# The condition's product with the modulation weights, on VectorE or on four column tiles of TensorE

## The chip, the cores and the metric

The kernel runs on one core of one Trainium2 chip. The metric is the device time of one execution in microseconds (us); of several runs the median is taken. The engines are named as in the profile: PE is TensorE (PEld its weight loads), DVE is VectorE, ACT is ScalarE, POOL is GpSimd, SP is SyncE, whose queue issues most of the DMAs (SPq).

## What is computed

A two-layer trunk on 1024 frames of width 1024. Each layer has a mixer and a mixture of experts, and each of these is modulated by vectors that come from the condition `c`. Only this part of the reference bears on the change:

```python
cond = jax.nn.silu(c)                       # (1, 1024)
for i in range(2):
    shift1, scale1, gate1, shift2, scale2, gate2 = jnp.split(cond @ ada_w[i] + ada_b[i], 6, axis=-1)
    h = modulate(rmsnorm(x, norm_mix_w[i]), shift1, scale1)     # h * (1 + scale) + shift
    ...                                                         # mixer, experts
```

So there are twelve vectors of 1024 numbers, each the product of one vector of 1024 with a 1024 x 1024 block of float32 weights (4 MB): 48 MB of weights that are read once and used for one row.

## The kernel before, in words

`even` (line 1979) is layer 0 up to its experts. It goes through these stages, which overlap at their edges:

- **Start.** Four tiles of x are loaded, normed and transposed (`norm_S`, line 189). `ada` (line 142) makes scale1 and shift1 of layer 0 (line 2024). `modulate` (line 217) then writes the normed input as a high and a low part (hTh, hTl), and four more tiles follow.
- **Projections** (loop at line 2047, eight steps). Each step loads a block of `even_w_in`, splits it into a high and a low part (`wsplit`, line 228: ACT at line 138, then DVE at line 139) and multiplies it in three passes (`mm3`, lines 240 to 242). Within the steps n = 1 to 5, `ada` makes eight more vectors (line 2067): gate1, scale2, shift2, gate2 of layer 0 and shift1, scale1, gate1, scale2 of layer 1. A vector's loads and products are written into the code in one place and its last part (after the `yield` at line 169) at the next vector's place.
- **Stick-breaking attention and S5** (`stick`, line 283, and `s5_quad`, line 462), eight row blocks and four groups of channels.
- **GLU** (`glu`, line 586), with the last two vectors, shift2 and gate2 of layer 1 (line 2103), and some row blocks of `stick` beside it. Then the output projection and the routing.

`ada` takes each 1024 x 1024 block in four quarters h of 256 columns. `wload` (line 74) brings a quarter (1 MB) into a tile `w` of shape 128 x (8 row blocks k) x 256; its DMA is issued by SP. The tile comes from a ring of two buffers in the projection and GLU stages (`pick(1)`) and of four at the start, so a load waits in SP's queue until the products of an earlier quarter have read their buffer, and what stands behind it in that queue waits too. The products are made on DVE: one `tensor_scalar` (line 160) and seven `scalar_tensor_tensor` (line 167) that add w[:, k, :] times a column of `cs` (silu of c) into `adacc`, 128 x 256. After the `yield`, PE sums over the 128 partitions with `ones_f` (line 179, two products of one column for each quarter), DVE adds the bias (line 180), and for most vectors ACT's queue writes the result to DRAM (line 187). One quarter out of the eight at the start is done on PE instead, sixteen sums of eight products of one column each (`on_pe`, line 177).

The program is written with a tile framework. `tile.TileContext(nc, schedule_with_timeline_sim=True)` (in `kernel`) means that the order of the instructions on each engine is made by a planner that plays the program through on a simulated timeline and prefers work that stands earlier in the code; semaphores are put in by the framework. Each engine runs its list in order: an instruction that waits holds up all that stand behind it. `psum("e")` gives one of two PSUM banks that `ada`, `s5_quad` and `glu` share.

Of the kernel before, what the change touches and what calls it, by code (L numbers as in the profile page):

```python
# [9 lines left out]
FT = mybir.dt.float32  # L10
# [11 lines left out]
D = 1024  # L22
# [14 lines left out]
class Core:  # L37
# [41 lines left out]

    def consts(self):  # L80
        nc, c = self.nc, self.const
        ji = c.tile([128, 128], I32, name="ji")
        nc.gpsimd.iota(ji, pattern=[[1, 128]], base=0, channel_multiplier=-1)
        self.ident = c.tile([128, 128], FT, name="ident")
        nc.vector.tensor_scalar(self.ident, ji, 0.0, None, op0=OP.is_equal)
        self.ustrict = c.tile([128, 128], BF, name="ustrict")
        nc.vector.tensor_scalar(self.ustrict, ji, 0.0, None, op0=OP.is_gt)
        self.ones_b = c.tile([128, 128], BF, name="ones_b")
        nc.vector.memset(self.ones_b, 1.0)
        self.ones_f = c.tile([128, 128], FT, name="ones_f")  # L90
        nc.vector.memset(self.ones_f, 1.0)
        self.nhalf = c.tile([128, 16], FT, name="nhalf")
        nc.vector.memset(self.nhalf, -0.5)
        self.euler = c.tile([128, 4], FT, name="euler")
        nc.vector.memset(self.euler, math.e)
        self.eps = c.tile([128, 1], FT, name="eps")
        nc.vector.memset(self.eps, 1e-6)
        cr = c.tile([128, KD], FT, name="cr")
        nc.sync.dma_start(cr, self.a["c"][0].rearrange("(k p) -> p k", p=128))
        self.cs = c.tile([128, KD], FT, name="cs")  # L100
        nc.scalar.activation(self.cs, cr, AF.Silu)
        self.mod_d = self.dram.tile([2, 6, D], FT, name="mod_d")
        self.mod = {}

# [34 lines left out]
        self.nc.vector.tensor_tensor(lo, x, hi.bitcast(FT), op=OP.subtract)  # L139


    def ada(self, i, names, pool, tag, on_pe=((),), pool_eng=False):

        nc, a, c = self.nc, self.a, self.const
        order = ["shift1", "scale1", "gate1", "shift2", "scale2", "gate2"]
        aw, ab = a["ada_w"], a["ada_b"]
        for m, nm in enumerate(names):
            j = order.index(nm)
            b = self.col(pool, ab[i, j * D:(j + 1) * D], "adac", KD)
            keep = j < 2  # L150
            o = c.tile([128, KD], FT, name=f"{nm}_{i}") if keep else pool.tile([128, KD], FT, name="adao", bufs=2)
            parts = []
            for h in range(4):
                w = self.wload(aw[i, :, j * D + h * 256:j * D + (h + 1) * 256], 8)
                if h in on_pe[m % len(on_pe)]:
                    parts.append(w)
                    continue
                acc = pool.tile([128, 256], FT, name="adacc", bufs=4)
                eng = nc.gpsimd if pool_eng else nc.vector
                eng.tensor_scalar(acc, w[:, 0, :], self.cs[:, 0:1], None, op0=OP.mult)  # L160
                for k in range(1, KD):
                    wk, ck = w[:, k, :], self.cs[:, k:k + 1]
                    if pool_eng:
                        eng.tensor_scalar(wk, wk, ck, None, op0=OP.mult)
                        eng.tensor_tensor(acc, acc, wk, op=OP.add)
                    else:
                        eng.scalar_tensor_tensor(acc, wk, ck, acc, op0=OP.mult, op1=OP.add)  # L167
                parts.append(acc)
            yield
            pc = self.psum(tag)  # L170
            for h, x in enumerate(parts):
                for q in range(2):
                    qs = slice(q * 128, (q + 1) * 128)
                    p = pc[:, 2 * h + q:2 * h + q + 1]
                    if h in on_pe[m % len(on_pe)]:
                        for k in range(KD):
                            nc.tensor.matmul(p, x[:, k, qs], self.cs[:, k:k + 1], start=(k == 0), stop=(k == KD - 1))
                    else:
                        nc.tensor.matmul(p, x[:, qs], self.ones_f[:, 0:1], start=True, stop=True)
            nc.vector.tensor_tensor(o, pc[:, 0:KD], b, op=OP.add)  # L180
            if nm.startswith("scale"):
                n = self.col(pool, (a["norm_mix_w"] if nm == "scale1" else a["norm_ffn_w"])[i], "adan", KD)
                nc.vector.scalar_tensor_tensor(o, o, 1.0, n, op0=OP.add, op1=OP.mult)
            if keep:
                self.mod[nm, i] = o
            else:
                nc.scalar.dma_start(self.mod_d[i, j].rearrange("(k p) -> p k", p=128), o)
# [1791 lines left out]
    def even(self, x_src):  # L1979
# [9 lines left out]
        with self.banks("pse", b=4, a=1, d=1, e=2):  # L1989
# [16 lines left out]
            with tc.tile_pool(name="hT", bufs=1, side="right") as hp, tc.tile_pool(name="wsp", bufs=1, side="right") as wp:  # L2006
                hs = [hp.tile([128, KD, T], FR, name=n) for n in ("hTh", "hTl")]
                with tc.tile_pool(name="nrm", bufs=1, side="left") as np_:
# [12 lines left out]
                        load(t)  # L2021
                    pre = qT[:].rearrange("p h t -> p (h t)").rearrange("p (k t) -> p k t", k=KD)
                    self.norm_S(get, None, None, *hs, np_, "ad", range(4), eng=nc.gpsimd, pre=pre)
                    list(self.ada(0, ["scale1", "shift1"], ap, "e", ((2,), ())))
                    mod = self.mod["scale1", 0], self.mod["shift1", 0]
                    for h in range(2):
                        ts = slice(256 * h, 256 * h + 256)
# [157 lines left out]
```

## Time and profile before

| what | us |
|---|---|
| three runs, median (lowest to highest) | 3074.36 (3069.44 to 3075.93) |
| the profiled execution | 3069.93 |
| its span | 3068.1 |
| PE busy in the span | 2656.4 (87%) |
| DVE busy in the span | 1792.6 (58%) |

Between the span and the execution's own time lie 1.8 us. All of `ada` lies in the first 650 us of the span; the rest (the experts of layer 0, layer 1) uses its results only. The table shows averages over the whole span, so what bounds a stage has to be read from windows of the trace: for each stretch the busy time of each engine, the TensorE clock that was granted (1.00 is 2.4 GHz, 0.50 is 1.2 GHz) and the share of the DMA engines. A matmul in float32 stands in the trace as two entries, one for each of its passes; the duration of one entry reaches past the start of the next, so the pace is read from how far apart the starts lie.

### The profile page before, as it was taken

What the parts mean: (1) busy time and instruction counts of PE and PEld (TensorE: products, weight loads), DVE (VectorE), ACT (ScalarE), POOL (GpSimd) and SP (SyncE); (2) the same over time, 40 slices, a digit from 0 to 9 for tenths busy, and PEclk for the clock granted to TensorE, in tenths of its full rate; (3) what the DMA queues carried; (4) which work ended last, traced back from release to release, by engine and by line L of the source; (5) the groups of instructions that cost most, each with busy time, mean ns of one, the idle gap of its engine ahead of it and who ended that gap; (6) DMA issues with size and microseconds to landing.
All of it is one profiled execution on the core that took longest, in us unless ns stands there. A gap on an engine that the chain in (4) does not pass through costs nothing. (4 is left out here: it accounts for less than half of the span.)

```text
span 3068.1 us, 39923 instructions
## 1 busy us (share of the span) xinstructions
PE 2656.4 (87%) x14357; PEld 1854.7 (60%) x14357; DVE 1792.6 (58%) x3211; ACT 1120.7 (37%) x1777; POOL 831.2 (27%) x1157
## 2 busy tenths in 40 slices
PE   4987688989699999995799999999978799998991
PEld 4776466647444466662677777777877444566660
DVE  7546999655633477664734555646547434556664
ACT  4311456432232345552433323323233223345451
POOL 5260755324211031101301533354105111111101
PEclk9998689989799999997898978886988799999996
DMA  8746220223588899997745322244443689999995
GB/s 279 178 124 198 63 59 15 90 68 105 211 338 324 351 368 407 376 389 256 260 138 176 110 77 78 67 121 103 107 125 119 242 348 365 369 362 396 388 385 239
DMA packets 345018, 672.82 MB, mean 219 GB/s; under 512 B 118591, under 2 KB 259935, under 8 KB 293104
## 3 DMA queue, kind: packets, MB, share of 16 engines
q1 hardware_dynamic: 272960, 611.23, 54.7%
q10 hardware_dynamic: 56752, 25.41, 3.0%
q0 software_dynamic: 15104, 33.58, 3.0%
q8 instruction: 115, 1.88, 0.3%
q14 instruction: 87, 0.71, 0.1%
HBM read 611.31 MB, written 79.79 MB: 225 GB/s over the span
## 5 line engine op out<-in xcount | busy, mean ns | idle before, releaser
L139 DVE TENSOR_TENSOR wlo<-w,whi 128x1024 fp32r<-128x1024 f32 x384 | 451.4, 1220 | 114.0 <-ACT whi L138 112.3
L138 ACT ACTIVATE whi<-w 128x1024 fp32r<-128x1024 f32 x384 | 390.5, 1054 | 237.1 <-PE ps_g L839 69.9
L240 PE MATMUL ps_b<-hTh,wh 128*128 128x512 f32 x608 | 259.3, 428 | 28.2 <-ACT cc L1382 12.5
L241 PE MATMUL ps_b<-hTl,wh 128*128 128x512 f32 x608 | 255.2, 420 | 0.0
L242 PE MATMUL ps_b<-hTh,wl 128*128 128x512 f32 x608 | 254.8, 419 | 0.0
L788 POOL DMA_INDIRECT xg<-h_d,tok x56 | 80.6, 1440 | 641.6 <-PE ps_t L106 617.1
L847 DVE TENSOR_TENSOR hs<-hs,ps_u 128x512 f32<-128x512 f32 x48 | 32.9, 685 | 263.3 <-PE ps_u L917 212.4
L794 POOL DMA_INDIRECT ye_d<-y,tab x48 | 71.9, 1497 | 421.8 <-DVE y L856 328.4
L167 DVE SCALAR_TENSOR_TENSOR adacc<-w,cs,adacc 128x256 f32<-128x256 f32 x329 | 161.1, 507 | 5.2
L139 DVE TENSOR_TENSOR wl<-w,wh 128x1024 fp32r<-128x1024 f32 x84 | 104.0, 1253 | 97.3 <-ACT wh L138 88.1
L240 PEld LDWEIGHTS ps_b<-hTh,wh 128*128 128x128 f32 x608 | 124.8, 206 | 55.9 <-ACT cc L1382 13.3
L846 ACT ACTIVATE hs<-ps_g 128x512 f32<-128x512 f32 x48 | 28.7, 598 | 325.0 <-PE ps_g L917 244.8
L313 DVE TENSOR_TENSOR_SCAN sP<-keep,sP,sbz 128x256 f32<-128x256 f32 (+1 forms) x160 | 132.9, 874 | 21.7 <-POOL keep L307 10.5
L917 PE MATMUL ps_g<-w,xh 128*64 128x512 f32 x512 | 143.5, 598 | 0.0
L133 POOL TENSOR_TENSOR rs<-rm,nhalf 128x1 f32<-128x1 f32 (+2 forms) x56 | 49.9, 892 | 344.9 <-DVE rm L131 293.2
L138 ACT ACTIVATE wh<-w 128x1024 fp32r<-128x1024 f32 x84 | 86.3, 1053 | 150.5 <-PE ps_b L241 132.4
L241 PEld LDWEIGHTS ps_b<-hTl,wh 128*128 128x128 f32 x608 | 124.7, 205 | 27.2 <-DVE hTl L139 0.3
L242 PEld LDWEIGHTS ps_b<-hTh,wl 128*128 128x128 f32 x608 | 123.9, 204 | 28.3 <-issue 0.4
L917 PE MATMUL ps_u<-w,xh 128*64 128x512 f32 x512 | 137.6, 595 | 0.0
L315 POOL TENSOR_TENSOR sw<-sw,sP 128x512 f32<-128x512 f32 (+1 forms) x80 | 101.1, 1265 | 132.6 <-DVE sP L313 57.3
L926 PE MATMUL ps_y<-w,hh 128*64 128x512 f32 x512 | 122.0, 598 | 2.2 <-ACT hh L921 2.2
L1699 POOL TENSOR_TENSOR T<-N,X 128x60 f32<-128x60 f32 (+24 forms) x248 | 87.1, 351 | 125.2 <-DMA N<-n_d 93.3
(709 smaller groups left out, 6177.9 us busy)
## 6 DMA issues: line engine op xcount, KB each, us to landing
w<-in_moe_w_gate_dram SPq DMA_DIRECT2D x128, 1024.0 KB, 14.7
w<-in_moe_w_up_dram SPq DMA_DIRECT2D x128, 1024.0 KB, 14.8
w<-in_moe_w_down_dram SPq DMA_DIRECT2D x128, 1024.0 KB, 13.4
w<-in_ada_w_dram SPq DMA_DIRECT2D x48, 1024.0 KB, 5.8
w<-in_odd_w_in_dram SPq DMA_DIRECT2D x26, 1024.0 KB, 5.7
cy<-ye_d SPq DMA_DIRECT2D x16, 1024.0 KB, 10.8
cx<-xm_d SPq DMA_DIRECT2D x29, 512.0 KB, 7.5
w<-in_even_w_in_dram SPq DMA_DIRECT2D x8, 1024.0 KB, 8.5
```

What stands on the lines that cost most here:

```text
L138: self.nc.scalar.activation(hi, x, AF.Copy)
L139: self.nc.vector.tensor_tensor(lo, x, hi.bitcast(FT), op=OP.subtract)
L167: eng.scalar_tensor_tensor(acc, wk, ck, acc, op0=OP.mult, op1=OP.add)
L240: nc.tensor.matmul(p, a[0], b[0], start=first, stop=False)
L241: nc.tensor.matmul(p, a[0], b[1], start=False, stop=False)
L242: nc.tensor.matmul(p, a[1], b[0], start=False, stop=last)
L313: v.tensor_tensor_scan(P[:, r, 0:n][:, ::-1], keep[:, r, 0:n][:, ::-1], zero.to_broadcast([128, n]), P[:, r, n:n + 1], op0=OP.mult, op1=OP ...
L315: g.tensor_tensor(w[:, :, 0:n], w[:, :, 0:n], P[:, :, 1:n + 1], op=OP.mult)
L788: nc.gpsimd.indirect_dma_start(out=xg, out_offset=None, in_=h_d[:], in_offset=bass.IndirectOffsetOnAxis(ap=tokc, axis=0), bounds_check=T - ...
L917: nc.tensor.matmul(ps[z][r], x[:, 4 * h + k, r], w[z][h][:, k, :], start=(h == 0 and k == 0), stop=(h == 1 and k == 3))
L926: nc.tensor.matmul(py[n][r], ht[:, f, r], w[2][f // 2][:, f % 2, two[n]], start=(f == 0), stop=(f == 3))
L1699: g.tensor_tensor(o, N[:, 0:j, j:j + 1].to_broadcast([128, j, w]), X[:, j:j + 1, c:8].to_broadcast([128, j, w]), op=OP.mult)
```

## The change

The eight DVE instructions of a quarter go. In their place are eight matmuls on PE: the weights are `csz`, a new constant tile in which column 0 of 32 holds a column of `cs` and the others are zero, and the quarter's w[:, k, :] is the moving operand (256 columns). Row block k goes to the column tile k % 4 (`tile_position=(0, 32 * (k % 4))`), so that four row blocks write to four groups of 32 partitions of one PSUM bank, and k = 4 to 7 add to what k = 0 to 3 left. Two quarters share a bank (`pa`, from the same two banks "e"); ACT copies the bank to SBUF (`adacc`, now 128 x 512, two buffers in place of four of 128 x 256). The sum over partitions by `ones_f` stays as it was in kind, eight products of one column for each vector (now for all twelve vectors; `on_pe` is gone). The loads `w` and their rings stay.

```diff
     def consts(self):
-        ji = c.tile([128, 128], I32, name="ji")
+        self.ident = c.tile([128, 128], FT, name="ident")
+        ji = self.ident[:].bitcast(I32)
         nc.gpsimd.iota(ji, pattern=[[1, 128]], base=0, channel_multiplier=-1)
-        self.ident = c.tile([128, 128], FT, name="ident")
-        nc.vector.tensor_scalar(self.ident, ji, 0.0, None, op0=OP.is_equal)
         self.ustrict = c.tile([128, 128], BF, name="ustrict")
         nc.vector.tensor_scalar(self.ustrict, ji, 0.0, None, op0=OP.is_gt)
+        nc.vector.tensor_scalar(self.ident, ji, 0.0, None, op0=OP.is_equal)
...
+        self.csz = c.tile([128, KD, 32], FT, name="csz")
+        nc.vector.memset(self.csz, 0.0)
+        nc.vector.tensor_copy(self.csz[:, :, 0:1], self.cs[:, :, None])
...
-    def ada(self, i, names, pool, tag, on_pe=((),), pool_eng=False):
+    def ada(self, i, names, pool, tag):
...
             parts = []
-            for h in range(4):
-                w = self.wload(aw[i, :, j * D + h * 256:j * D + (h + 1) * 256], 8)
-                if h in on_pe[m % len(on_pe)]:
-                    parts.append(w)
-                    continue
-                acc = pool.tile([128, 256], FT, name="adacc", bufs=4)
-                eng = nc.gpsimd if pool_eng else nc.vector
-                eng.tensor_scalar(acc, w[:, 0, :], self.cs[:, 0:1], None, op0=OP.mult)
-                for k in range(1, KD):
-                    wk, ck = w[:, k, :], self.cs[:, k:k + 1]
...
-                        eng.scalar_tensor_tensor(acc, wk, ck, acc, op0=OP.mult, op1=OP.add)
+            for h2 in range(2):
+                pa = self.psum(tag)
+                for h in (2 * h2, 2 * h2 + 1):
+                    w = self.wload(aw[i, :, j * D + h * 256:j * D + (h + 1) * 256], 8)
+                    for k in range(KD):
+                        q = 32 * (k % 4)
+                        nc.tensor.matmul(pa[q:q + 32, h % 2 * 256:h % 2 * 256 + 256], self.csz[:, k, :], w[:, k, :],
+                                         start=(k < 4), stop=(k >= 4), tile_position=(0, q))
+                acc = pool.tile([128, 512], FT, name="adacc", bufs=2)
+                nc.scalar.activation(acc, pa, AF.Copy)
                 parts.append(acc)
             yield
             pc = self.psum(tag)
-            for h, x in enumerate(parts):
-                for q in range(2):
...
-                    if h in on_pe[m % len(on_pe)]:
-                        for k in range(KD):
-                            nc.tensor.matmul(p, x[:, k, qs], self.cs[:, k:k + 1], start=(k == 0), stop=(k == KD - 1))
-                    else:
-                        nc.tensor.matmul(p, x[:, qs], self.ones_f[:, 0:1], start=True, stop=True)
+            for n in range(KD):
+                nc.tensor.matmul(pc[:, n:n + 1], parts[n // 4][:, n % 4 * 128:n % 4 * 128 + 128], self.ones_f[:, 0:1], start=True, stop=True)
...
-                    list(self.ada(0, ["scale1", "shift1"], ap, "e", ((2,), ())))
+                    list(self.ada(0, ["scale1", "shift1"], ap, "e"))
```

## Rows read from the trace of the kernel before

**Rows 1.** The page's part 1: busy time, share of the span and instructions of each engine over the whole span.

```profile
PE 2656.4 (87%) x14357; PEld 1854.7 (60%) x14357; DVE 1792.6 (58%) x3211; ACT 1120.7 (37%) x1777; POOL 831.2 (27%) x1157
```

**Rows 2.** Busy time of each engine (x instructions) in six stretches that follow the stages, then granted clock, DMA share and GB/s. The number behind the stretch is its length.

```profile
core 0: us, PE busy (x) PEld busy (x) DVE busy (x) ACT busy (x) POOL busy (x), PEclk, DMA share, GB/s
0.00:60.00 60.00, 23.17 (x100) 20.51 (x100) 43.23 (x90) 24.33 (x40) 35.83 (x27) 1.00 0.96 314
60.00:285.00 225.00, 207.22 (x909) 170.35 (x909) 131.70 (x357) 47.44 (x60) 65.67 (x180) 0.94 0.64 170
285.00:300.00 15.00, 3.61 (x15) 2.25 (x14) 4.68 (x16) 1.02 (x1) 5.03 (x7) 0.66 0.55 64
300.00:330.00 30.00, 15.05 (x66) 9.40 (x66) 26.53 (x55) 9.22 (x17) 19.45 (x20) 0.50 0.52 141
330.00:550.00 220.00, 178.55 (x1250) 127.63 (x1250) 212.49 (x362) 124.79 (x265) 131.84 (x122) 0.87 0.15 43
550.00:680.00 130.00, 113.50 (x618) 76.06 (x619) 73.22 (x124) 49.61 (x91) 33.87 (x45) 0.88 0.26 78
```

**Rows 3.** The same stretches for the DVE instructions of line 167 (seven of the eight of a quarter) alone.

```profile
285.00:300.00 15.00, 3.77 (x8) 0.66 0.55 64
300.00:330.00 30.00, 8.25 (x16) 0.50 0.52 141
330.00:550.00 220.00, 14.97 (x26) 0.87 0.15 43
550.00:680.00 130.00, 11.98 (x28) 0.88 0.26 78
sum 680.00, DVE 161.12; mean DVE 26.85
```

**Rows 4.** The same for line 160 (the first of the eight).

```profile
285.00:300.00 15.00, 0.85 (x1) 0.66 0.55 64
300.00:330.00 30.00, 1.19 (x3) 0.50 0.52 141
330.00:550.00 220.00, 2.24 (x3) 0.87 0.15 43
sum 680.00, DVE 21.36; mean DVE 3.56
```

**Rows 5.** Instructions in order of time at the start (start, us, engine, line, operation, tiles; in brackets the idle time of the engine before it and what ended it).

```profile
28.61 4.67 SPq L77 DMA_DIRECT2D w<-in_ada_w_dram x2
34.87 5.26 SPq L77 DMA_DIRECT2D w<-in_even_w_in_dram x2
43.56 2.00 ACT L138 ACTIVATE wh<-w 128x1024 fp32r<-128x1024 f32 x2 [5.38 <-DMA w<-in_even_w_in_dram]
44.21 0.35 DVE L160 TENSOR_SCALAR adacc<-w,cs 128x256 f32<-128x256 f32 x1
49.80 1.02 PE L179 MATMUL ps_e<-ones_f,adacc 128*128 128x1 f32 x4 [3.00 <-DVE adacc L167]
50.86 0.17 DVE L180 TENSOR_TENSOR shift<-ps_e,adac 128x8 f32<-128x8 f32 x1
60.40 1.22 PE L240 MATMUL ps_b<-hTh,wh 128*128 128x512 f32 x2 [9.58 <-ACT hTh L138]
```

**Rows 6.** PE in the stretch 60 to 285 by line and tiles (x entries, busy, mean ns of one, idle time before them and what ended it).

```profile
L240 PE MATMUL ps_b<-hTh,wh 128*128 128x512 f32 x192 | 80.7, 423 | 15.7 <-ACT hTh L138 9.6 <-ACT c L383 3.6 <-ACT ut L261 2.5
L179 PE MATMUL ps_e<-ones_f,adacc 128*128 128x1 f32 x112 | 15.5, 253 | 9.0 <-DVE adacc L167 9.0
```

**Rows 7.** Waits of DVE for a quarter's load (in total, times, longest), in the stretches 110 to 200 and 200 to 275.

```profile
DVE adacc L160 <- DMA w<-in_ada_w_dram: 19.8, 5, 10.2
...
DVE adacc L160 <- DMA w<-in_ada_w_dram: 28.1, 10, 8.6
```

**Rows 8.** Waits of SP's queue in the first 700 us: its loads (line 77) for the buffers that the DVE sums release.

```profile
SPq L77 <- DVE adacc L167: 211.7, 37, 27.3
```

**Rows 9.** The end of the projections and the start of the attention: one stretch of 10 us with all engines, and the DVE and PE instructions that waited longest there.

```profile
290.00:300.00 10.00, 2.05 (x8) 1.31 (x8) 0.00 (x0) 0.00 (x0) 0.03 (x1) 0.50 0.65 91
...
301.47 0.35 DVE L160 TENSOR_SCALAR adacc<-w,cs 128x256 f32<-128x256 f32 x1 [11.58 <-DMA w<-in_ada_w_dram]
...
306.11 1.01 PE L179 MATMUL ps_e<-ones_f,adacc 128*128 128x1 f32 x4 [14.06 <-DVE adacc L167]
323.45 1.01 PE L179 MATMUL ps_e<-ones_f,adacc 128*128 128x1 f32 x4 [5.40 <-DVE adacc L167]
```

**Rows 10.** The GLU stage: two stretches of 10 us with all engines, and a PE instruction that waited there.

```profile
570.00:580.00 10.00, 10.00 (x60) 7.04 (x59) 3.85 (x6) 5.59 (x11) 1.86 (x3) 1.00 0.01 2
600.00:610.00 10.00, 10.00 (x59) 7.01 (x59) 3.05 (x5) 3.98 (x8) 2.62 (x4) 1.00 0.55 112
...
622.12 0.80 PE L240 MATMUL ps_e<-gyh,gwh 128*128 128x512 f32 x1 [5.59 <-DVE gl L609]
```

**Rows 11.** Runs of float32 matmuls in order of time: line 531 with 128 weight columns and 256 moving columns, line 681 with 128 and 512, line 917 with 64 weight columns in two column tiles that take turns and 512, line 1087 with 32 weight columns in one tile and 192.

```profile
342.85 2.00 PE L531 MATMUL ps_e<-CA,br 128*128 128x256 f32 x8
684.61 3.60 PE L681 MATMUL ps_e<-w,gl 128*128 128x512 f32 x8
850.90 3.65 PE L917 MATMUL ps_g<-w,xh 128*64 128x512 f32 x16
720.32 0.84 PE L1087 MATMUL ps_b<-q_w,r_o 128*32 128x192 f32 x4
```

**Rows 12.** ACT from 60 to 700 us: copies of a whole PSUM bank to SBUF, by form; and PE from 0 to 680 us: the one quarter that is done on PE before.

```profile
L322 ACT ACTIVATE swT<-ps_a 128x512 f32<-128x512 f32 x64 | 38.4, 600 | 116.4 <-PE ps_a L106 91.8 <-issue 7.1 <-DVE bb L338 6.5
...
L177 PE MATMUL ps_e<-cs,w 128*128 128x1 f32 x32 | 7.0, 348 | 0.0
```

More of the change, by code (lines that the diff above doesn't have):

```diff
@@ L146, in ada @@
         aw, ab = a["ada_w"], a["ada_b"]
-        for m, nm in enumerate(names):
+        for nm in names:
             j = order.index(nm)
@@ L152, in ada @@
             parts = []
-            for h in range(4):
-                w = self.wload(aw[i, :, j * D + h * 256:j * D + (h + 1) * 256], 8)
-                if h in on_pe[m % len(on_pe)]:
-                    parts.append(w)
-                    continue
-                acc = pool.tile([128, 256], FT, name="adacc", bufs=4)
-                eng = nc.gpsimd if pool_eng else nc.vector
-                eng.tensor_scalar(acc, w[:, 0, :], self.cs[:, 0:1], None, op0=OP.mult)
-                for k in range(1, KD):
-                    wk, ck = w[:, k, :], self.cs[:, k:k + 1]
-                    if pool_eng:
-                        eng.tensor_scalar(wk, wk, ck, None, op0=OP.mult)
-                        eng.tensor_tensor(acc, acc, wk, op=OP.add)
-                    else:
-                        eng.scalar_tensor_tensor(acc, wk, ck, acc, op0=OP.mult, op1=OP.add)
+            for h2 in range(2):
[8 more added lines that the diff above has]
+                nc.scalar.activation(acc, pa, AF.Copy)
                 parts.append(acc)
@@ L170, in ada @@
             pc = self.psum(tag)
-            for h, x in enumerate(parts):
-                for q in range(2):
-                    qs = slice(q * 128, (q + 1) * 128)
-                    p = pc[:, 2 * h + q:2 * h + q + 1]
-                    if h in on_pe[m % len(on_pe)]:
-                        for k in range(KD):
-                            nc.tensor.matmul(p, x[:, k, qs], self.cs[:, k:k + 1], start=(k == 0), stop=(k == KD - 1))
-                    else:
-                        nc.tensor.matmul(p, x[:, qs], self.ones_f[:, 0:1], start=True, stop=True)
+            for n in range(KD):
+                nc.tensor.matmul(pc[:, n:n + 1], parts[n // 4][:, n % 4 * 128:n % 4 * 128 + 128], self.ones_f[:, 0:1], start=True, stop=True)
             nc.vector.tensor_tensor(o, pc[:, 0:KD], b, op=OP.add)
```

## The prediction

> **What bounds the kernel now.** I read the busy times of the whole span first, then the same by stage, then the waits and single instructions around `ada`. Over the span PE is the busiest engine and DVE has room [rows 1], which seems to speak against moving work to PE; but `ada` lies in the first 650 us only, so its stages decide. There the bound changes [rows 2]. From 0 to 60 us the DMA engines are full (0.96) and PE works 23 us of 60. From 60 to 285 (projections) PE works 207.2 of 225. From 285 to 330 nothing is full: PE works 18.7 of 45, at the lower clock towards the end (0.50 is 1.2 GHz). From 330 to 550 (attention and S5) DVE works 212.5 of 220 and PE 178.6. From 550 to 680 PE leads, with whole stretches at 10.0 of 10 [rows 2, 10]. DVE's sums for `ada` take 161.1 + 21.4 = 182.5 us [rows 3, 4], most of it in the first two stages, where DVE is not the bound. So the question is what eight PE products for a quarter cost where PE is the bound, and what 182.5 us less on DVE give back where DVE is.
>
> **The price of a quarter on PE.** Each float32 product is two entries: one quarter was done with 16 products, 32 entries [rows 12]. Eight products of 256 columns are 16 entries. At 128 weight columns, eight entries of 256 take 2.00 us, the last of them about 0.38, so starts lie (2.00 - 0.38) / 7 = 0.231 us apart [rows 11]. Narrow weights alone save nothing: 32 columns in one tile go at (0.84 - 0.35) / 3 = 0.163 us for 192 columns, 0.85 ns a column against 0.90 [rows 11]. Running side by side does: eight entries of 512 at full width take 3.60 us, and sixteen in two tiles of 64 take 3.65 [rows 11], so the second tile is free. Four tiles no row shows. Bounds for a quarter: all one after the other, 16 x 0.231 = 3.7 us; in pairs, 1.85; in fours, 0.92. Nearest is the pair row, whose second tile cost 1%; I take fours, and add the 0.15 by which the last entry outlasts the pace: **1.1 us a quarter**.
>
> The Trainium skill speaks against the full factor: "TensorE: Matmul & The Clock Gate", Part 3, "Measured speedup vs the span model", has 2.38 for three column tiles of 32. No run here shows three or four tiles; for two, the trace shows nearly the full factor (3.65 against 3.60 us for twice the entries). The result that the page would give is the third rival.
>
> **The change part by part**, against the profiled execution (3069.93 us, of which 3068.1 is span).
>
> *Start.* Today shift1 is ready at 51.0 and the first projection starts at 60.4, having waited 9.58 us for the modulated input [rows 5]. The last load of shift1 was issued ahead of the first `even_w_in` load, which had landed by 43.6 [rows 5]; at 314 GB/s [rows 2] 1 MB takes 3.3 us, so it was there at about 40.2, and DVE was behind with its sums (last quarter begun at 44.2). With PE: 40.2 + 1.1 + copy 0.60 [rows 12] + the last four entries 1.02 + bias 0.17 [rows 5] = 43.1, and PE has room (the quarter of line 177, 7.0 us, goes too [rows 12]). Since the loads may fall in another order I count 7 of these 7.9 us, and 1 more because DVE no longer mixes sums into the modulation: **-8**, between -3 and -11. The new constant and the reordering of `ident` fall before the first transpose, on an idle DVE: 0.
>
> *Projections.* 8 vectors, 32 quarters x 1.1 = 35.2 us. PE is idle 17.8 of 225 there, but in stalls and not as room for work (9.0 waiting for DVE's sums, 9.6 for the start [rows 6], part of which lies ahead of 60), so the whole of it lies on the path: **+35**, between +29 (in fours, no tail) and +59 (pairs). What follows the products is as before: eight products of one column a vector (line 179).
> Now the wait. DVE today stood 19.8 + 28.1 = 47.9 us waiting for loads [rows 7], and it could afford that; PE's own waits for the sums were 9.0 [rows 6]. In the changed kernel the product waits for the load on PE itself, and behind it stand the projections; ACT's copy waits for the product, and behind that stand the splits of the next projection weights, for which DVE and then PE wait, and the evictions that free PSUM. Against that, the 182.5 / 47 = 3.9 us that DVE takes for a quarter after its load has landed go, and SP's loads, which waited 211.7 us for the DVE sums to free buffers [rows 8], go out earlier. I set the new waits equal to the old, **0**, between -9 (all gone) and +24 (half of DVE's 47.9 now on PE). The copies are two a vector, 24 x 0.60 = 14.4 us on an ACT busy 47 of 225 [rows 2, 12]: hidden.
> A vector now takes three turns on the two banks "e" where it took one; the third turn waits for a copy of 0.60, and a half-filled bank that waits for a load in the S5 stage would take one of two from `s5_quad`: 0, up to +10.
>
> *The tail of `ada`, 285 to 330.* The projections are over, but the last sums are not. PE waits 14.06 and 5.40 us for them in front of attention work [rows 9], behind a load that DVE waited 11.58 for; for 10 us the engines do almost nothing [rows 9]. DVE's other work in these 45 us is 4.68 + 26.53 - 3.77 - 8.25 - 0.85 - 1.19 = 17.2 us [rows 2 to 4]. With the products inside the PE order of the projections and that stage 35 us longer, the loads should be through by its end; what is left is 17.2 of DVE work and about 4 to fill the chain: 45 - 21 = **-24**, between -12 (the late load stays late) and -28.
>
> *Attention and S5, 330 to 550.* DVE is the bound, and 14.97 + 2.24 = 17.2 us of its work go [rows 3, 4]. Next is PE, 178.6 in the remaining 203, 88%, so it still fits: **-17**, between -10 and -17.
>
> *GLU, 550 to 680.* Eight quarters, 8.8 us, in a stage where PE is full for most of the time; against it the 5.59 us in which PE waited for line 609 on DVE, which stands among the sums [rows 10]: **+4**, between -5 and +9.
>
> Sum: -8 + 35 + 0 - 24 - 17 + 4 = **-10**, so 3060 for the profiled execution. The median of the three runs lies 4.4 above that execution; I predict 3061, between -10 from the one and from the other. Everything after 680 us uses the results only and is taken as unchanged.
>
> **The rivals.**
> 1. *Slower: the tiles do not run four at a time.* In pairs a quarter costs 2.0, so 40 quarters (32 + 8) add 36 us: 3060 + 36 = 3096. One after the other, 3.7 + 0.15, adds 110: 3170. It turns at 10 / 40 = 0.25 more, that is 1.35 us a quarter: above that the kernel is slower. For it: no row has four tiles. Against: the second tile is free.
> 2. *Slower: PE takes over DVE's waits for loads.* Half of 47.9 on PE: 3060 + 24 = 3084, or 3096 if the late load of the tail stays too. For it: DVE waited 15 times from 110 to 275. Against: buffers come free sooner.
> 3. *No change: the fours overlap imperfectly,* at 0.8 of the full factor: 0.92 / 0.8 + 0.15 = 1.3, so +0.2 x 40 = +8: 3068. The page named above gives this factor (2.38 of 3).
> 4. *Faster still:* the old waits of 9.0 go and are not replaced, the full 11 at the start come, and the GLU gains 5: 3060 - 9 - 3 - 9 = 3039.
>
> **How the numbers follow.** Forecast 0.45 (its own range 3045 to 3075), rival 1 0.15, rival 2 0.15, rival 3 0.10, rival 4 0.15. Against the median of 3074.36, a change of 0.2% (6 us, about what a measurement of this kernel can tell from none) puts the borders at 3068 and 3080. Of the forecast's 0.45, 0.35 is faster, 0.08 the same, 0.02 slower. Faster: 0.35 + 0.15 = 0.50; same: 0.08 + 0.10 = 0.18; slower: 0.02 + 0.15 + 0.15 = 0.32. The range from 3032 to 3104 takes in rival 4, both forms of rival 2 and the pairs of rival 1, and leaves out the serial tiles and sums in which several ends meet.
>
> **What would show it.** In the trace after: the starts of the new matmuls, four at once and then 0.23 us, against two or one; the first projection at about 52 instead of 60.4; PE's waits on the load of `ada_w` between 60 and the end of the projections (9 or less, against 24 and more); whether the 10 idle us at the end of the projections are gone; DVE's busy time in the attention stage, full but 17 us shorter. I am wrong if the projections grow by more than 60 us, or if the attention stage does not shrink when its DVE work does: then it was a chain and not DVE that bounded it.

## The result, and the profile after

The changed kernel takes 3104.93 us (median of four runs, 3100.55 to 3110.52); the kernel before, with one run more beside it, 3071.9 (3069.24 to 3075.93). The ratio is 1.0114, with a 95% interval of 1.0093 to 1.0134: slower by some 33 us, where 10 us less were forecast. The profiled execution took 3110.52 (span 3108.4).

The whole-span line (part 1 of the page of the changed kernel) moved as the change says, against [rows 1]: DVE lost 162.5 us, PE gained 41.5.

```profile
PE 2697.9 (87%) x15097; PEld 1857.8 (60%) x15097; DVE 1630.1 (52%) x2838; ACT 1132.6 (36%) x1800; POOL 806.1 (26%) x1157
```

To see where, the first layer is cut where its stages really end in each kernel: first projection product, last projection group, last S5 product, last GLU product, first load of expert weights. The kernel before by these stages (busy time of each engine, clock, DMA share, GB/s):

```profile
60.40:284.20 223.80, 206.42 (x907) 170.05 (x907) 130.52 (x354) 47.04 (x59) 64.92 (x179) 0.94 0.64 170
284.20:537.80 253.60, 189.95 (x1271) 134.82 (x1270) 236.75 (x419) 124.08 (x263) 151.86 (x143) 0.80 0.21 52
537.80:636.80 99.00, 86.77 (x488) 60.01 (x488) 63.67 (x108) 42.57 (x77) 27.47 (x29) 0.93 0.29 90
636.80:805.10 168.30, 151.28 (x766) 107.87 (x764) 100.02 (x323) 50.87 (x84) 62.01 (x61) 0.93 0.26 85
```

and the changed one:

```profile
54.50:325.70 271.20, 244.99 (x1418) 182.34 (x1419) 38.98 (x133) 55.45 (x74) 56.30 (x178) 0.93 0.59 157
325.70:541.40 215.70, 164.41 (x1139) 120.10 (x1138) 195.62 (x338) 108.95 (x234) 134.01 (x130) 0.87 0.10 22
541.40:651.50 110.10, 102.36 (x701) 67.43 (x700) 62.28 (x92) 53.70 (x100) 31.73 (x36) 0.97 0.37 119
651.50:820.30 168.80, 155.75 (x814) 110.50 (x812) 105.87 (x328) 55.41 (x93) 65.06 (x65) 0.94 0.26 85
```

Read down the lengths: start 60.4 to 54.5 (-5.9), projections 223.8 to 271.2 (+47.4), attention and S5 253.6 to 215.7 (-37.9), GLU 99.0 to 110.1 (+11.1), the rest +0.5. The first layer loses 15.2 us. The forecast had -8, +35, -41 and +4.

In the projections PE now waits for the weights themselves (waits of PE in that stage of the changed kernel), in place of the 9.0 us for DVE's sums [rows 6]:

```profile
PE ps_e L164 <- DMA w<-in_ada_w_dram: 20.1, 5, 6.9
PE ps_b L233 <- ACT hTh L142: 10.5, 1, 10.5
PE ps_b L233 <- ACT ut L254: 5.3, 2, 3.3
```

SP's loads wait for the products to free their buffers (first 700 us), where they had waited 211.7 us for DVE's sums [rows 8]:

```profile
SPq L77 <- PE ps_e L164: 156.9, 39, 20.7
```

The products themselves are as quick as hoped. Three of them in order of time (16 entries are a quarter, 32 two quarters in a row):

```profile
29.10 1.07 PE L164 MATMUL ps_e<-w,csz 128*32 128x256 f32 x16 [1.58 <-DMA w<-in_ada_w_dram]
...
169.87 1.93 PE L164 MATMUL ps_e<-w,csz 128*32 128x256 f32 x32
...
215.94 1.93 PE L164 MATMUL ps_e<-w,csz 128*32 128x256 f32 x16 [6.91 <-DMA w<-in_ada_w_dram]
```

1.07 us a quarter, 1.93 for two; the last line took 1.93 for one, after a wait of 6.91. All 512 entries of the stage are busy for 38.3 us, and 38.3 + 20.1 - 9.0 = 49.4 is, within 2 us, what the stage grew by.

The rest of the loss lies far from the change. From the first load of expert weights to about 2020 us the two traces run side by side; then the changed kernel falls behind by another 20 us, in the recurrence of the second layer's mixer, whose code is the same. The kernel before, from the first load of `odd_w_in` to the last state product, in two stretches:

```profile
1426.80:2007.00 580.20, 520.41 (x3347) 402.90 (x3347) 311.87 (x538) 205.32 (x384) 180.50 (x367) 0.85 0.42 135
2007.00:2281.10 274.10, 251.13 (x2083) 217.21 (x2081) 139.45 (x271) 80.79 (x217) 84.10 (x187) 0.83 0.43 107
```

and the changed kernel, cut after the same 580.2 us:

```profile
1440.20:2020.40 580.20, 520.75 (x3348) 403.32 (x3349) 311.42 (x538) 205.24 (x384) 179.74 (x366) 0.85 0.43 135
2020.40:2314.70 294.30, 256.65 (x2085) 220.76 (x2085) 138.27 (x273) 82.15 (x219) 83.16 (x192) 0.80 0.37 100
```

274.1 became 294.3 with nearly the same number of instructions. PE idles 37.7 us there instead of 23.0 and its clock falls from 0.83 to 0.80. Its longest waits in the second stretch, first before, then after (lines 681 and 674 are the same line of code):

```profile
PE ps_o L681 <- DVE om L684: 4.5, 2, 2.3
PE ps_a L106 <- DVE yq L1815: 4.5, 2, 4.3
```

```profile
PE ps_o L674 <- DVE om L677: 14.7, 4, 8.8
PE ps_b L110 <- ACT my L1510: 6.4, 2, 5.2
```

The planner wrote another order. Compared by line and tile over the second layer's mixer (5428 PE entries before, 5432 after), a few entries differ at about 1908 us of the kernel before; from 2038 us on the two lists part, and some 760 entries in all stand in another place. The profiled execution was also 6.7 us slower in the second experts (793.7 against 787.0 us). That part ranged from 784.6 to 798.0 over all runs but the one with false vectors (e4); it too goes with the order (788.8 in e3, which has the order of before, 794.5 in e12, which has that of after).

### The profile page after: what moved, and what is told of

Its sections match the earlier page's. It is cut to its first block, busy times and chain, and to the rows that moved or that the text cites. A ratio compares the mean times of both kernels' runs of the same rounds, so it can differ in the third digit from the quotient of the medians.

```text
span 3108.4 us, 41090 instructions
## 1 busy us (share of the span) xinstructions
PE 2697.9 (87%) x15097; PEld 1857.8 (60%) x15097; DVE 1630.1 (52%) x2838; ACT 1132.6 (36%) x1800; POOL 806.1 (26%) x1157
## 5 line engine op out<-in xcount | busy, mean ns | idle before, releaser
L781 POOL DMA_INDIRECT xg<-h_d,tok x56 | 87.7, 1566 | 643.1 <-PE ps_t L110 610.5
L787 POOL DMA_INDIRECT ye_d<-y,tab x48 | 61.2, 1275 | 428.4 <-DVE y L849 344.9
L306 DVE TENSOR_TENSOR_SCAN sP<-keep,sP,sbz 128x256 f32<-128x256 f32 (+1 forms) x160 | 141.4, 925 | 48.7 <-ACT keep L293 30.2
L839 ACT ACTIVATE hs<-ps_g 128x512 f32<-128x512 f32 x48 | 28.7, 598 | 337.9 <-PE ps_g L910 258.0
L110 PE MATMUL ps_t<-ident,xg 128*128 128x128 f32 (+1 forms) x448 | 76.1, 305 | 42.9 <-issue 17.6
## 6 DMA issues: line engine op xcount, KB each, us to landing
w<-in_moe_w_down_dram SPq DMA_DIRECT2D x128, 1024.0 KB, 12.4
```

Of the source, the lines that this page charges most:

```text
L110: self.nc.tensor.transpose(out, in_, self.ident[:n, :n])
L306: v.tensor_tensor_scan(P[:, r, 0:n][:, ::-1], keep[:, r, 0:n][:, ::-1], zero.to_broadcast([128, n]), P[:, r, n:n + 1], op0=OP.mult, op1=OP ...
L781: nc.gpsimd.indirect_dma_start(out=xg, out_offset=None, in_=h_d[:], in_offset=bass.IndirectOffsetOnAxis(ap=tokc, axis=0), bounds_check=T - ...
```

## The experiments

Three points on the span are used: the first load of expert weights (805.1 before, 820.4 after) ends the first layer's mixer; from the first load of `odd_w_in` to the last state product is the **second mixer** (854.3 before, 874.6 after); the medians are compared with those of the kernel before on the same chip (3070.0 for e1 to e4, 3086.2 for e5 to e8, 3078.7 for e9 to e11, 3090.0 for e12). So one kernel differs by 20 us between chips, and stages of runs on different chips can be compared only roughly; the nineteen executions on the chip of e1 to e4 alone range from 3063.7 to 3076.7. e6, e7 and e8 are single executions, without an interval.

**e1, e2: the same edit to both kernels, after which the planner writes the same second layer for both.**

```diff
                 nc.gpsimd.memset(R["G"], 0.0)
+                nc.vector.memset(R["G"], 0.0)
```

> The kernel before with one line more: in the second layer, the state tile G that GpSimd clears is cleared a second time by VectorE (128x512, half a microsecond of work). It makes the planner write the second layer's recurrence in another order (1181 of 1684 TensorE instructions of that part stand elsewhere). Theory A (the loss of the change is two things: some 14 us in the first layer, and 17 us in the second layer because the planner wrote another order there): up to the first load of expert weights the time is that of before within 2 us (805 us), and the second layer alone moves, by anything from -20 to +20 us. Theory B (the order of the second layer costs nothing by itself; its loss in the changed kernel comes from what the change does to clock or transfers): total within 4 us of before.

> The changed kernel with the same extra line. The planner now writes the second layer in the same order as for the kernel before with that line, instruction for instruction on all five engines. Theory A: this kernel lies 13 to 16 us above the kernel before with that line (all of it there by the first load of expert weights at 820 us) and nothing is added afterwards. Theory B: it lies 33 us above it, as the change lies above the kernel before, and 17 us of that appear after 2020 us.

e1: 3051.67 us, ratio 0.9951 (0.9929 to 0.9973): a line that does nothing useful makes the kernel *before* faster by 15 us (8 to 22). Expert load at 800.8, 4.3 ahead of the trace of before where A allowed 2, with the first layer's order unchanged; second mixer 842.7 instead of 854.3. Theory B fell: the second layer's time moves with no change in the first. Whether the new order did it or the line itself, this run does not tell; e11 below has the line without a new order. e2: 3080.4 us, 1.0034 (1.0021 to 1.0046), so 28.7 above e1 by the medians and 23.8 by the spans, where A said 13 to 16 and B 33. The place is A's: expert load 18.5 behind e1, second mixer 847.9, 5.2 behind e1 and not 20.3. Its sizes were too small. The second stretch of the mixer, e1 and then e2:

```profile
2000.00:2263.70 263.70, 244.46 (x2051) 210.58 (x2050) 141.05 (x274) 82.33 (x217) 76.71 (x170) 0.83 0.43 113
```

```profile
2025.20:2289.00 263.80, 243.84 (x2038) 210.16 (x2039) 141.06 (x274) 81.73 (x216) 75.00 (x164) 0.83 0.43 112
```

The cuts lie 579.1 and 584.1 us into the mixer, at nearly the same place in the list. With one order the stretch takes 263.7 and 263.8 us, without the change and with it. The stretch that had differed by 20 us no longer does.

**e3: the changed kernel, its vectors spread otherwise, with the order of the kernel before.**

```diff
-                    for _ in range((0, 1, 1, 2, 2, 2, 0, 0)[n]):
+                    for _ in range((1, 1, 1, 1, 2, 2, 0, 0)[n]):
```

> The changed kernel with its eight vectors of the projection stage spread as 1, 1, 1, 1, 2, 2 over the first six projection blocks instead of 0, 1, 1, 2, 2, 2. The planner writes the second layer as it does for the kernel before. Theory A: the second layer's 17 us are gone; the first layer loses 8 to 16 us against before, so the total is 3080 to 3090. Theory B: 3098 to 3108.

3080.19 us, 1.0032 (1.0014 to 1.005): theory A. The second mixer takes 856.5, within 2.2 of the kernel before, whose order it has, and its second stretch (cut after 580.2 us again) is

```profile
2013.50:2289.70 276.20, 250.79 (x2056) 217.62 (x2057) 138.29 (x270) 80.49 (x215) 80.58 (x179) 0.82 0.41 106
```

against 274.1 and 294.3. The expert load starts at 811.5: spreading the vectors also gave 9 of the first layer's 15 us back.

**e4: products without their loads.** For the eight vectors of the projection stage `data` is `hTh[:, :, 0:256]`.

```diff
                     w = self.wload(aw[i, :, j * D + h * 256:j * D + (h + 1) * 256], 8)
+                    if data is not None:
...
+                        nc.gpsimd.tensor_copy(seen, w[:, KD - 1, 255:256])
+                        w = data
```

> The changed kernel in which the products of the eight vectors of the projection stage read 256 columns of the resident modulated input instead of the loaded weights; the loads stay, and GpSimd copies one column of each when it lands, which frees its buffer. Those eight modulation vectors are therefore not those of the reference. TensorE cannot wait for a load of ada_w in the projections any more. Read up to 680 us only (the planner's order of the second layer is another one). Theory A1 (the excess over my 35 us in the projections is TensorE waiting for these loads, 20 us in the changed kernel): the projection stage shortens from 271 us to 250 to 256. Theory A2 (the waits only stand in for others: buffers, evictions, ScalarE's copies): it stays above 264.

The stage takes 240.6 us (58.2 to 298.8), 30.6 less than in the changed kernel: A1, and more than A1 asked for. The group of all products of the stage, whose idle time no longer names a load:

```profile
L169 PE MATMUL ps_e<-hTh,csz 128*32 128x256 f32 x512 | 31.5, 382 | 2.3 <-DVE shift L178 1.6 <-ACT adacc L172 0.7
```

The expert load starts at 788.3, 12 to 17 us ahead of the kernel before. Its total (3182.87) says nothing: with false modulation vectors the tokens go to other experts, and the stretch from the expert load to `odd_w_in` grew from about 620 to 701 us. My later expectations name 2395 as an upper end for planner orders; that number comes from this and is void as such.

**e5: the same products, asked for earlier.** A generator goes through the 32 quarters: one after every 24 projection products, and with it the load of the quarter after next is issued (the first two loads ahead of the loop).

```diff
+        for n, (i, nm, h) in enumerate(qs):
...
+            w = box.pop(n)
             for k in range(KD):
                 q = 32 * (k % 4)
                 nc.tensor.matmul(pa[q:q + 32, ...], self.csz[:, k, :], w[:, k, :], ..., tile_position=(0, q))
+            fetch(n + 2)
...
+            yield
...
     def proj_T(self, w, col, hs, tag, out_cb):
...
+            if self.tick is not None:
+                next(self.tick, None)
```

> The changed kernel with the same products, but the 32 quarters of the projection stage stand one by one between the groups of projection products (after every 24 of them), each with its load issued two quarters earlier, instead of four or eight quarters in a row behind their loads. Same number of products and loads. The planner writes the second layer in an order that no kernel here has had, so the reading is the first layer: start of the first load of expert weights, 805 and 801 us in the kernel before and in it with the extra line, 820 and 819 in the changed one. Theory A1 (the products fit; what the change loses in the first layer is TensorE waiting for loads that are asked for too late): 785 to 800, the projection stage 240 to 252 us. Theory A2 (the product work itself does not fit beside the projections): 812 to 822, the stage 262 and more.

A1 again, now with every product and load in place: the stage takes 245.9 us and the expert load starts at 793.6. The stage, and PE's wait for the loads in it:

```profile
54.40:300.30 245.90, 237.22 (x1402) 174.94 (x1403) 38.63 (x133) 54.58 (x73) 56.50 (x178) 0.97 0.62 169
```

```profile
PE ps_e L205 <- DMA w<-in_ada_w_dram: 7.7, 2, 5.0
```

e5 changes two things at once, when the loads are asked for and that the products stand one quarter at a time; e4, with the products still in a row, shows that the wait is what counts, but which of the two shortens it was not tried alone. The wait fell by 12.4 us and the stage by 25.3; PE was busy 7.8 us less for the same work, at a clock of 0.97 instead of 0.93. The total is 3079.14 us, 0.9989 (0.9967 to 1.0011): no change. Its second mixer, in yet another order, takes 871.7; the kernel before was not traced on that chip.

**e6: without the tiles.**

```diff
-                        nc.tensor.matmul(pa[q:q + 32, ...], self.csz[:, k, :], w[:, k, :],
-                                         start=(k < 4), stop=(k >= 4), tile_position=(0, q))
+                        nc.tensor.matmul(pa[0:32, ...], self.csz[:, k, :], w[:, k, :],
+                                         start=(k == 0), stop=(k == KD - 1))
...
```

> The changed kernel without the tiles: all eight products of a quarter go to the same 32 columns of TensorE and are summed there. Read in the first layer alone. By the prediction's bound of 3.7 us a quarter against 1.1 and the whole of it on the path: projections 271 + 32 x 2.6 = 354 us, first expert load 820 + 40 x 2.6 = 924. If waits for loads cover part of the products in the changed kernel, less: the projections at 320 to 345.

The stage takes 352.4 us (expected 354), the expert load starts at 933.8 (expected 924); one execution, 3239.78 us. Two quarters in a row:

```profile
150.62 7.09 PE L164 MATMUL ps_e<-w,csz 128*32 128x256 f32 x32
```

7.09 against 1.93 us: the tiles are worth a factor of 3.67, and the waits for loads cover none of the added product time (PE still waits 30.0 us for them).

**e7: the start and the last two vectors on PE, six and the GLU's two on DVE. e8: all but the GLU's two on PE.** The new argument is true for a vector on PE; the diff is e7's, and e8 has `True` in its first place.

```diff
-                        late = [self.ada(i, [nm], ap, "e")]
+                        late = [self.ada(i, [nm], ap, "e", len(todo) < 2)]
...
-                        late = self.ada(1, [todo.pop(0)], ap, "e")
+                        late = self.ada(1, [todo.pop(0)], ap, "e", False)
```

> TensorE does the products of four vectors alone: the two at the start and the last two of the projection stage; VectorE sums the other six and the two of the GLU as before (into halves of the 128x512 tile). Read in the first layer. Theory A (the prediction's terms hold one by one: start -6 as measured, tail and attention stage -10 to -40, projections +9): first expert load 770 to 795. If the gain of the attention stage needs all sums gone from VectorE: 797 to 805.

> The changed kernel with the two vectors of the GLU stage summed on VectorE as before, all others on TensorE. Read in the first layer. If the eleven us that the GLU stage grew by are its eight quarters on TensorE: the stage is back at 99 to 103 us and the first expert load at 809 to 813. If they are attention work that slid into it: the stage stays at 106 to 110 us.

Both missed, and both for the same reason. e7 (3132.91): expert load at 825.5. e8 (3130.08): 850.1. The DVE sums of the GLU vectors do not stay in the GLU. Attention and S5 and then the GLU in e8, DVE instructions that touch `adacc` (columns: PE, PEld, DVE, ACT):

```profile
336.10:571.70 235.60, 1.84 (x16) 1.94 (x16) 17.56 (x32) 0.00 (x0) 0.84 0.15 39
571.70:666.70 95.00, 1.84 (x16) 1.94 (x16) 15.54 (x32) 0.00 (x0) 0.95 0.31 93
```

The planner puts one vector's 32 sums into the attention stage, where DVE is busy 223.37 of the 235.6 us. Against e5 on the same chip (whose three stages lie within 4 us of the changed kernel's), that stage grows from 217.3 to 235.6, the GLU shrinks from 110.8 to 95.0, and the stage behind it grows from 165.1 to 183.3. So the two GLU vectors on PE are worth 493.3 against 513.9 us from the last projection to the expert load, 20.6 us. Their eight quarters cost 10 us of PE in the GLU stage and pay back more beside it. In e7 PE waits 18.7 us for the sums left on DVE in the projections (9.0 before) and 9.8 for a late load in the attention stage; the prediction's terms do not add up one by one when only some vectors move.

**e9, e10, e11: e5 with the line of e1, with a vector finished at once (the diff below), and with both.**

```diff
-            if last is not None:
-                self.ada_end(*last, pool, tag)
-                last = None
             if h == 3:
-                last = (i, nm, parts)
+                self.ada_end(i, nm, parts, pool, tag)
...
```

> The interleaved kernel with the extra clearing of the state tile on VectorE. Its first layer is the interleaved one's: first expert load at 788 to 798 us. The planner's order of its second layer is new again. Theory A (from the first expert load on, the time belongs to the order that the planner wrote, 2249 to 2395 us in the runs so far): it cannot be told from the first layer; if the extra line helps here as it helped the kernel before (2249 against 2263), the total is 3045 to 3060, a ratio of 0.990 to 0.996 to the kernel before; if it gets one of the slow orders, over 3090. Theory B (the interleaved kernel's second layer follows from its own first layer): 2279 again within 5 us, total 3072.

> The interleaved kernel with one step moved: the eight narrow products, the bias and the store of a finished vector come right after its last quarter, not one quarter later. In the first layer TensorE may wait 0.6 us for ScalarE's copy, eight times: at most 5 us, first expert load 790 to 800. The planner's order of the second layer is another one. Theory A: from the first expert load on anything from 2249 to 2395 us. Theory B: 2279 within 5.

> Both edits: the vector finished at once, and the extra clearing of the state tile. First expert load at 790 to 800. A fourth order of the second layer for nearly the same first layer. Theory A: the four interleaved kernels differ by 10 us and more from each other after the first expert load while their first layers agree within 8 us. Theory B: they agree within 5 us there.

e9: 3064.33 us, 0.9957 (0.994 to 0.9974), by the ratios faster than both kernels; e10: 3095.1, 1.0048 (1.0032 to 1.0064); e11: 3089.65, 1.004 (1.0027 to 1.0052). Their expert loads start at 791.0, 799.3 and 796.6, as expected. Theory B (2279 us from there on) fell: 2271.1, 2302.0 and 2291.1. A's claim of 10 us between each two did not hold either (e5 and e9 differ by 7.6): the second mixers take 865.3, 876.7 and 864.6 (e5 871.7), and the line that was worth 11.6 us in e1 is worth 6.4 in e9. The rest lies in the experts (786.3, 797.8, 795.2 in the second ones). At their start PE of e10 and e11 stands 10.9 us, that of e5 and e9 2.7 and 2.5. The kernel before stands 11.3 us at the same place and e6 and e7 11.2, so the wait goes with the order; why is open. Nor is e11's a fourth order: e10's second layer is in the order of e6 and e7, and e11's is the same but for the extra line.

**e12: the copies on VectorE.**

```diff
-                nc.scalar.activation(acc, pa, AF.Copy)
+                nc.vector.tensor_copy(acc, pa)
```

> The changed kernel with the copies of the products (24 of 128x512) on VectorE instead of ScalarE. The planner writes the second layer exactly as for the changed kernel. First question, ScalarE's order: its copies wait 95 us for products in the projection stage, and the splits of the next weights stand behind them. If that holds up TensorE, its waits for loads or evictions shrink and the projection stage falls by 5 us or more, first expert load 808 to 815. If ScalarE was early anyway (the copies wait, but TensorE never waits for a split there): 271 us and 816 to 822 as in the changed kernel. Second question, the order of the second layer: from the first load of odd_w_in to its last state product the changed kernel takes 874.6 us where the kernel before takes 854.3; theory A says 870 to 879 for the same order, a theory by which that was an accident of the one execution says 850 to 862.

3114.95 us, 1.0074 (1.0048 to 1.0099). The stage takes 279.3 us and the expert load starts at 828.8, 8 us later than in the changed kernel and outside both expectations: nothing gained, so ScalarE's order was not what held PE, whose wait for the loads was 26.7 us there. The second mixer takes 870.6 (expected 870 to 879), with the stretch

```profile
2030.00:2320.80 290.80, 249.15 (x2060) 215.63 (x2059) 138.33 (x272) 81.59 (x217) 81.15 (x184) 0.81 0.39 101
```

against 294.3 for the changed kernel, whose order it has.

**The second mixer, by order.** Kernels with one and the same order in the traces, by line and tile on all five engines and but for a handful of entries, stand in one row:

| order written for | second mixer, us | expert load to the end, us | first layer up to the expert load, us |
|---|---|---|---|
| before, e3 | 854.3, 856.5 | 2263.0, 2267.0 | 805.1, 811.5 |
| after, e12 | 874.6, 870.6 | 2288.1, 2286.5 | 820.4, 828.8 |
| e1, e2 | 842.7, 847.9 | 2249.0, 2254.4 | 800.8, 819.3 |
| e6, e7, e10 | 877.8, 879.2, 876.7 | 2304.2, 2305.6, 2302.0 | 933.8, 825.5, 799.3 |
| e11 (that of e10 and one line more) | 864.6 | 2291.1 | 796.6 |
| e5; e9; e8 (one each) | 871.7; 865.3; 869.1 | 2278.7; 2271.1; 2278.2 | 793.6; 791.0; 850.1 |

Within a row the mixer agrees to 5.2 us and the whole rest of the kernel to 5.4, though the first layers differ by up to 135; between rows the mixer spans 37 and the rest 57. On one chip alone, e6 and e7 lie 25 to 27 us above e5 and e8 from the expert load on.

e11 shows how far such a trace can be trusted: nothing but one line of half a microsecond parts its second mixer from e10's, yet it is 12.1 us shorter. Most of that lies in one stretch, the same 300 PE entries in e10 and then in e11:

```profile
1824.90:1866.90 42.00, 42.00 (x300) 33.26 (x300) 17.44 (x35) 9.00 (x17) 15.77 (x44) 0.68 0.27 77
```

```profile
1826.00:1857.00 31.00, 30.83 (x300) 24.85 (x299) 15.97 (x33) 8.04 (x16) 12.13 (x30) 0.97 0.36 101
```

PE is busy throughout in both; the granted clock is 0.68 in the one and 0.97 in the other. By medians e10 and e11 differ by 5.5 us, with overlapping intervals of the ratio, so the line without a new order is not shown to be worth anything. And a difference of some 12 us between two single traces need not come from the order.

## Why the prediction was wrong

Two steps failed. **"I set the new waits equal to the old, 0"** is the first, and by itself it takes the gain away. The mechanism that I gave rival 2 (PE takes over DVE's waits) held in the first layer: PE waits 20.1 us for the loads where it had waited 9.0, and the first layer came out 15.2 us slower, which on the profiled 3069.93 is 3085. That this is rival 2's 3084 is in part luck: rival 2 put 24 us on the wait, which grew by 11.1, and the rest of the miss comes from other terms (summed below). My reason against it, that buffers come free sooner, was too weak: SP's loads still stood 156.9 us for buffers, where it had been 211.7; the code asked for a quarter's load right ahead of its products, four or eight quarters in a row on two buffers, and PE reached them as early as the loads did. DVE could stand in front of a load without holding up the projections; PE cannot. e4 and e5 show it from both sides: without the wait, or with loads asked for two quarters ahead, the stage takes 240.6 and 245.9 us, that is +17 and +22 on the 223.8 of before, less than the forecast's +35.

**"Everything after 680 us ... is taken as unchanged"** is the second. It computes the same, but the planner orders the whole program at once, and another first layer gave the second layer another order. In the traces that is 20.3 of the 40.3 us between the two spans. By the totals it is smaller: after against before is 33 us, e2 against e1, with one order for both, 25 to 29. So of the 33 us I put 15 to 19 to the first layer (805.1 and 800.8 before, 820.4 and 819.3 after), which leaves 14 to 18 for the order and the spread between executions together. How much of it is the order stays open: 4 to 8 by e1 and e2 (33 less 25 to 29), about 16 by e3 (25 us below the changed kernel by the ratios, 8.9 of them in the first layer), 20.3 by the two second mixers, which are single traces. That the time behind the expert load goes with the order is shown by the rows of the table; why one order is slower than another was not tried, and the kernel before was not run in the order of the changed kernel.

The other steps:

- *Price of a quarter, 1.1 us*: 1.07 measured; rivals 1 and 3 are out. "TensorE: Matmul & The Clock Gate" of the Trainium skill, Part 3, "Measured speedup vs the span model", has 2.38 for three column tiles, a fifth lost. Here four tiles of 32 columns and 256 moving columns give 3.67, and the measurement decides for this shape. With the slow quarters after waits all 32 of the stage come to 38.3 us, 1.2 each, where 35.2 were counted; without waits (e4) to 31.5.
- *Start, -8*: -5.9, inside its bounds; first projection at 54.5 where 52 was named.
- *Tail and attention, -24 and -17*: together -37.9 for -41. The idle stretch of [rows 9] is gone (PE is busy 15.00 of the 15 us from 285 to 300), and the attention stage shrank with DVE's work, from 236.75 busy to 195.62. So DVE was the bound there, as said; e8 agrees, where 17.56 us of sums put back lengthen the stage by 18.3. What is missing to 41 is less than one new wait at its start, 11.4 us of PE for an S5 table (`cl`) that ACT's queue loads.
- *Banks "e", ACT's copies, 0*: in the first 650 us of the changed kernel PE waits once for a copy, 1.0 us, and not in the projections; e12 gained nothing.
- *GLU, +4*: +11.1. The products were sized about right (10.0 us for 8.8). What was missed is attention work. PE's three attention groups in that stage, before:

```profile
L297 PE MATMUL ps_b<-kT,qT 64*128 64x256 f32 (+1 forms) x72 | 13.0, 438 | 0.9 <-ACT sw L302 0.9
L326 PE MATMUL ps_d<-swT,v 128*64 128x128 f32 x136 | 12.4, 305 | 1.9 <-ACT swT L322 1.9
L106 PE MATMUL ps_a<-ident,sw 128*128 128x128 f32 x68 | 12.3, 305 | 0.0
```

and after, with the products:

```profile
L290 PE MATMUL ps_b<-kT,qT 64*128 64x256 f32 (+1 forms) x96 | 16.2, 415 | 0.7 <-ACT sw L295 0.7
L319 PE MATMUL ps_d<-swT,v 128*64 128x128 f32 x176 | 15.2, 290 | 2.9 <-ACT swT L315 2.8
L110 PE MATMUL ps_a<-ident,sw 128*128 128x128 f32 x88 | 14.9, 288 | 0.0
L164 PE MATMUL ps_e<-w,csz 128*32 128x256 f32 x128 | 10.0, 384 | 1.3 <-DMA w<-in_ada_w_dram 1.3
```

46.3 us of attention where 37.7 had been: when S5 ended earlier, more of the attention was left for the GLU stage. I had split one balance at a border that moves.

Summed, the first layer missed by 2.1 (start) + 12.4 (projections) + 3.1 (attention) + 7.1 (GLU) + 0.5 = 25.2 us, from -10 to +15.2.

## What to carry to other kernels

When work moves from an engine with slack to the one that bounds the stage, its wait for data moves with it: price the wait at the old engine's own waits until the loads are shown to be early, and move the loads' issue together with the work (here two quarters ahead and one quarter at a time, which turned a first layer 15 us slower than before into one 7 to 14 us faster in e5 and e9). Where one planner orders the whole program, an edit early on reshuffles stages far behind it. Compare such kernels stage by stage, at points that both have, and look whether the instruction order behind the edit is the same before calling the total the edit's doing. A harmless line that moves the total by 0.5% (e1) is the size of what was being tested here.

## What the runs showed of the hardware

- Four column tiles of 32, float32, 256 moving columns: 32 entries in 1.93 us against 7.09 on one tile, 0.92 of the full factor of four.
- Longer waits on PE went with a lower granted clock and more busy time in the same stage. With waits of 20.1 us for loads the projection stage ran at 0.93 and PE was busy 245.0 us; with 7.7 us (e5) at 0.97 and 237.2; with none (e4) at 0.98 and 228.1, for 1418, 1402 and 1418 entries. It is no strict rule: e3 has 22.7 us of waits, 0.94 and 241.1. Around the wait of 6.91 us the clock was 1.00 from 205 to 209 us and 0.50 from 214 to 222, and the 16 entries after the wait took 1.93 us instead of 1.07.
- The clock can also differ with PE busy throughout: the same 300 entries took 42.0 us at 0.68 in e10 and 31.0 us at 0.97 in e11. What decides it there is not shown.
